# A memory layer's sample keys and values, turned on VectorE and gathered on GpSimd instead of transposed on TensorE

## The chip, the cores and the metric

The kernel runs on one core of one Trainium2 chip. The metric is the device time of one launch in microseconds (us), lower is better; a kernel's time is the median of its runs. The kernel before takes 877.05 us (three runs, 877.02 to 877.51). In what follows PE is TensorE, DVE VectorE, ACT ScalarE, POOL GpSimd and SP SyncE, which here issues loads and stores.

## The reference

One inference step of a two-layer decoder: 256 prompt tokens of one new sequence, and 64 sample tokens (8 sequences of 8 tokens), which carry states along. Layer 0 mixes tokens with a gated MLP, layer 1 with an mLSTM memory of 8 heads (keys of 128, values of 256 numbers); a convolutional FFN follows each. The change lies in layer 1. For each head and chunk the reference computes (cut):

```python
sc  = einsum('bhtd,bhsd->bhts', qc, kc) * w_intra          # scores
num = w_inter[..., None] * einsum('bhtd,bhde->bhte', qc, C) \
    + einsum('bhts,bhse->bhte', sc, vc)
den = w_inter * einsum('bhtd,bhd->bht', qc, n) + sum(sc, -1)
h   = num / maximum(abs(den), exp(-m_t))[..., None]
kg  = kc * g[..., None]
C_new = decay * C + einsum('bhsd,bhse->bhde', kg, vc)      # the state update sums over tokens
```

Then each head's output is normalised, multiplied by `sigmoid(o)` and projected. The state update and `sc @ v` sum over tokens, so that keys and values are needed with tokens on the partitions, while the projections deliver them with features on the partitions.

## The kernel before

All activations lie with features on the 128 partitions and the T = 320 tokens (256 of the prompt, then 64 of the sample) along the row. A weight matrix is worked in output blocks of 128 rows; `block()` multiplies one by up to eight 128-row pieces of the activations in three passes (high part by high part, low by high, high by low), each matmul 128x320 into one PSUM bank. The raw weights come by SP's queue, ACT makes the high part `wh` (line 178), DVE the low part `wl` (line 179). PE runs these passes from the start to the end of the program.

PSUM has eight banks: a ring of three (`psm`, tile `pm`) and one of five (`psa`). A block takes the next bank of `psm`; so does the second matmul of most pairs `pcs` of the state update, and in heads 1 to 6 `pk`. The next owner of a bank waits until the last one's readers are done.

`layer_b` runs over the heads h = 0 to 7. The iteration of head h works on its own projections and finishes head h-1. On PE, for heads 2 to 6: q block, k block, `inter`(h-1) (old state by q), `numer`(h-1) (scores by values), first v block, `state_prompt`(h-1) (`pCp`), a pair `pcs` of the sample's state update, second v block, more `pcs`, `scores`(h) (`psc`), first o block, `pcs`, second o block, `finish`(h-1) (six transposes `phn` of the normalised output, line 1102), `pcs`, then `k_nat`(h) and `v_nat`(h): three transposes of k (`pk`) and six of v (`pv`), two tiles of prompt tokens and one of sample tokens each. Head 1 has its first v block ahead of `inter`, and its first o block ahead of `scores`. Heads 4 to 6 hold eight early blocks of the output projection. Beside it:

- `qk_epi`: scale by the norm (`bpad`), convolution (`bcv`, one step on ACT, three on DVE), Tanh (`bth`), then `qs` (lines 849 and 851, prompt and sample apart), with a second copy of the sample's 64 columns (line 857) for k, and the splits `qh`, `qhl`, `kh`, `khl`.
- `v_epi`: ACT copies a v block from PSUM to `vTb` (line 868), and the sample's columns once more (line 869).
- `scores`: `w`, `Qz`, then `Pf` on DVE, split into `Ph`, `Pl` and, for the sample, `Ps`.
- `v_nat`: `vh` on ACT (line 932), `vl` and the sample's lower half of `vh` on DVE (line 935), `vb` on ACT. `k_nat`: the sample's gated keys `kgs` (961 ACT, 962 DVE), POOL's masked copies `kgz` (985), the prompt's `kgh`, `kgl`.
- `stats`: `dn` on ACT, moments `mv`, then `rd`, `t1` on DVE, `sl` on POOL; `normed`: `nb` on DVE, `hn` on ACT. `state_sample`: DVE adds `pcs` to a state tile `C` (line 1081), SP stores it. `o_epi`: `o_b` on DVE (line 1089), `th_o` on ACT. `finish`: `y_b` on DVE (lines 1105 and 1106, prompt and sample apart), split into `yhb`, `ylb`.

PE's order is the program's, pinned by `mm` and `tr`. On the other engines a scheduler sets it from the dependences, with edges given by hand: `behind(a, b)` puts a after b on their engine without a wait, `issue_after` does so for all that a block of code issues.

Of the kernel before, what the change touches and what calls it, by code (L numbers as in the profile page):

```python
# [11 lines left out]
F32 = mybir.dt.float32  # L12
F32R = mybir.dt.float32r
AF = mybir.ActivationFunctionType
# [17 lines left out]
CW = DV + 2  # L32
HV = 160


# [24 lines left out]
class Net:  # L60
# [627 lines left out]
    def layer_b(self):  # L688
# [5 lines left out]
        with ExitStack() as ctx:  # L694
# [24 lines left out]


            def gates(rp):

# [108 lines left out]
            def qk_epi(h, j, ps):  # L831
# [16 lines left out]
                qs = lp.tile([P, 384], F32, tag="qs", name="qs", bufs=2)  # L848
                q_ = nc.vector.scalar_tensor_tensor(qs[:, :TP], th[:, :TP], 1.0, cv[:, :TP], op0=ADD, op1=MULT)
                tv, c_ = [x[:, 256:].rearrange("p (b e) -> p b e", e=11)[:, :, 3:11] for x in (th, cv)]  # L850
                s["q_"] = q_, nc.vector.scalar_tensor_tensor(seg(qs[:, TP:T]), tv, 1.0, c_, op0=ADD, op1=MULT)
                nm = "kh" if j else "qh"
# [3 lines left out]
                if j:  # L856
                    nc.scalar.copy(qs[:, T:384], qs[:, TP:T])
                if j:
                    self.split(hh, ll, qs[:, :n])
                else:  # L860
                    self.split_y(hh, ll, qs[:, :n])
                s["hi"] = self.parts[0]
                s["qk"[j]] = (qs, hh, ll)
                return self.parts[1]

            def v_epi(h, j, ps):
                vT = lp.tile([P, 384], F32, tag="vT", name="vTb", bufs=2)
                nc.scalar.copy(vT[:, :T], ps[:, :T])
                made = nc.scalar.copy(vT[:, T:384], ps[:, TP:T])
# [9 lines left out]
            def scores(h):  # L879
# [28 lines left out]
                Qd = Qz[:, NS:].rearrange("p (b e) -> p b e", e=32)[:, :, :NS]  # L908
                nc.vector.scalar_tensor_tensor(Qd, seg(q[:, TP:T]), 0.5, seg(pb[:, T:384]), op0=MULT, op1=MULT)
                Pf = hp.tile([P, 448], F32, tag="Pf", name="Pf", bufs=1)  # L910
# [7 lines left out]
                both = Ps.rearrange("p i (j e) -> p i j e", e=32)[:, :, :, :16]  # L918
                nc.scalar.copy(both[64:], both[:64])
                s["P"] = (Ph, Pl, dec)  # L920

            def v_nat(h):
                s = S[h]
                pv = [self.psa.tile([P, 512], F32, tag="pa", name="pv") for _ in range(2)]
                dsts = [pv[t // 2][:, (t % 2) * DV:] for t in range(3)]
                for t in range(3):
                    for e in range(2):
                        self.tr(dsts[t][:, e * P:(e + 1) * P], s["vT"][e][:, t * P:(t + 1) * P], self.ident)
                for t in range(3):
                    dst = dsts[t]  # L930
                    sc = self.rc[:, t:t + 1]
                    nc.scalar.activation(vh[:, t, :, :P], parity(dst[:, :DV]), AF.Copy, scale=sc)

                    r, out = (slice(0, P), vl[:, t, :, :P]) if t < 2 else (slice(64, P), vh[64:, t, :, :P])
                    low = nc.vector.scalar_tensor_tensor(out, parity(dst[r, :DV]), sc[r], vh[r, t, :, :P].bitcast(F32), op0=MULT, op1=SUB)
                    if t == 1:
                        self.v_low = low

                nc.scalar.copy(vb[:, :, :P], vh[:, 2, :, :P])
                self.vb_made = nc.scalar.copy(vb[:32, :, :P], vh[32:64, 2, :, :P])  # L940

            def v_first(h):

                nc.scalar.copy(vh[32:64, 2, :, :P], vh[:32, 2, :, :P])

            def k_nat(h):
# [10 lines left out]
                g = colsT[:, 2, 32 + h:33 + h]  # L957
                src = pk[:, 2 * P:3 * P]

                for i, (r, o) in enumerate(((slice(0, 32), slice(32, 64)), (slice(32, 64), slice(0, 32)))):  # L960
                    nc.scalar.activation(kgs[:, i, :], src, AF.Copy, scale=g)
                    s["ks"] = nc.vector.scalar_tensor_tensor(kgs[o, i, :], src[r], g[r], kgs[r, i, :].bitcast(F32), op0=MULT, op1=SUB)
# [3 lines left out]

                def prompt():
                    for t in range(2):
                        g = colsT[:, t, 32 + h:33 + h]
                        src = pk[:, t * P:(t + 1) * P]  # L970
                        nc.scalar.activation(kgh[:, t, :], src, AF.Copy, scale=g)
                        nc.vector.scalar_tensor_tensor(kgl[:, t, :], src, g, kgh[:, t, :].bitcast(F32), op0=MULT, op1=SUB)

# [4 lines left out]
            def k_mask(h):  # L978
                _, _, kgs, kgz = S[h]["kg"]
                if h == NH - 1:  # L980
                    for b in range(NB):
                        nc.scalar.activation(kgz[:, b, :], kgs[:, b // 4, :].bitcast(F32), AF.Copy, scale=mk[:, b:b + 1])
# [37 lines left out]
            def stats(h, between=None):  # L1020
                s = S[h]
                num, mv, dn = s.pop("num"), mvs[h % 2], dns[h % 2]
                v_first(h)
                for t in range(3):
                    nc.scalar.activation(dn[:, t:t + 1], num[t][:, DV:DV + 1], AF.Abs)
                bst = hp.tile([P, 3, 6], F32, tag="bstat", name="bstat", bufs=1)
                for t in range(3):
                    nc.vector.bn_stats(bst[:, t, :], num[t][:, :DV])
                    nc.vector.bn_aggr(mv[:, t, :], bst[:, t:t + 1, :])
# [6 lines left out]
                sl = hp.tile([P, 3], F32, tag="sl", name="sl", bufs=1)  # L1036
                nc.gpsimd.tensor_tensor(sl, t1, self.mhalf.to_broadcast([P, 3]), op=ALU.pow)
                s["norm"] = num, mv, sl
# [4 lines left out]
            def normed(h):  # L1043
# [5 lines left out]
                for t in range(3):  # L1049
                    if h == NH - 1 and t:  # L1050
                        nc.vector.tensor_scalar(hn[:, t, :], src[t][:, :DV], mv[:, t, 0:1], sl[:, t:t + 1], op0=SUB, op1=MULT)
                    else:
                        nc.scalar.activation(hn[:, t, :], src[t][:, :DV], AF.Identity, scale=sl[:, t:t + 1], bias=nb[:, t:t + 1])
# [41 lines left out]
            def finish(h):  # L1095
# [3 lines left out]
                for e in range(2):  # L1099
                    pt = self.psa.tile([P, 512], F32, tag="pa", name="phn")  # L1100
                    for t in range(3):
                        self.tr(pt[:, t * P:(t + 1) * P], hn[:, t, e * P:(e + 1) * P], self.ident)
                    y = self.tp.tile([P, T], F32, tag="yf", name="y_b", bufs=2)
                    o = s["o"][e]
                    nc.vector.scalar_tensor_tensor(y[:, :TP], o[:, :TP], 1.0, pt[:, :TP], op0=ADD, op1=MULT)
                    nc.vector.scalar_tensor_tensor(pairs(y[:, TP:]), pairs(o[:, TP:]), 1.0, apart(pt[:, TP:384]), op0=ADD, op1=MULT)
                    g = gnh[:, 2 * h + e:2 * h + e + 1]
                    yp, h2, l2 = parity(y), halves(yh[:, e, :]), halves(yl[:, e, :])
                    nc.scalar.activation(h2, yp, AF.Copy, scale=g)
                    s.setdefault("yl", []).append(nc.vector.scalar_tensor_tensor(l2, yp, g, h2.bitcast(F32), op0=MULT, op1=SUB))  # L1110
# [129 lines left out]
            begin(0)  # L1240
            self.prefetch(0, self.used + 2)
            begin(1)
            inter(h)
            numer(h)
            ps = blk()

            def between():
                with tc.issue_after(self.t_made.ins):
                    self.prefetch(0, self.used + 2)
                o_epi(h, 0, ps)  # L1250

# [89 lines left out]
def _lay_out(i):  # L1341
# [28 lines left out]
    w = i["b_w_in"][0]  # L1370
    a["b_win"] = _blocks(w[:, :48 * P], order)
    g = np.zeros((P, 2 * P), w.dtype)
# [64 lines left out]
```

## Time and profile before

| | |
|---|---|
| median of three runs | 877.05 us |
| the profiled execution | 876.92 us, its span 875.2 us |
| memory layer, head 1's q block to head 7's | 412.0 to 587.9 us |
| busy: PE, DVE, ACT, POOL | 869.1, 671.8, 506.0, 143.0 us |
| PE's clock granted | full in all slices |
| one wl split (DVE), one wh split (ACT) | 1.18 and 1.01 us, 254 of each |
| a weight matmul 128x320 | 0.30 us each, one every 0.136 us |

Matmuls overlap in the array: a row of the timeline shows each with its whole duration, and what a matmul costs is the distance to the next one's start. In the timeline a row is: start, duration, engine, line, operation, output <- inputs, shape, count; in brackets stands the idle time before it and what ended it. A busy engine that is never the last to be waited for costs nothing.

### The profile page before, as it was taken

To read this page: it belongs to the slowest core of one execution; us is meant where nothing else is said; L and a number is where in the kernel's file an instruction comes from. 1 tells how busy PE (TensorE), PEld (TensorE's weight loads), DVE (VectorE), ACT (ScalarE), POOL (GpSimd) and SP (SyncE) were. 2 spreads that over 40 slices of the span, in tenths; PEclk is the share of its full clock that TensorE was granted. 3 is DMA by queue.
4 is the path that set the end of the run, shared out by engine and by line. 5 is a ranking of instruction groups with operands and counts; after the bars stand their busy time and mean duration, and the time that the engine had idled before them with its cause. 6 is when DMAs were issued, how large, how long until landed. Compare 5 with 4: busy or idle time off the path is not lost.

```text
span 875.2 us, 16934 instructions
## 1 busy us (share of the span) xinstructions
PE 869.1 (99%) x6388; PEld 852.2 (97%) x6388; DVE 671.8 (77%) x1302; ACT 506.0 (58%) x917; POOL 143.0 (16%) x297
## 2 busy tenths in 40 slices
PE   9999999999999999999999999999999999999997
PEld 7899999999999999999999999999999999999997
DVE  7766986588878865559999997878998888786443
ACT  7557554455555543447877776656766555554442
POOL 3530000031000000005433232313003000000000
PEclk9999999999999999999999999999999999999999
DMA  8855645545445555555746777565664554455551
GB/s 264 259 170 167 183 145 180 170 155 171 156 158 169 162 167 157 158 185 150 241 152 225 242 232 219 184 215 170 197 219 145 170 169 149 165 163 166 156 153 60
DMA packets 54949, 155.74 MB, mean 178 GB/s; under 512 B 7460, under 2 KB 12716, under 8 KB 54868
## 3 DMA queue, kind: packets, MB, share of 16 engines
q1 hardware_dynamic: 54868, 154.67, 55.7%
q8 instruction: 50, 0.82, 0.4%
q14 instruction: 31, 0.25, 0.1%
HBM read 142.66 MB, written 11.99 MB: 177 GB/s over the span
## 4 chain that ended last, share of the span: by engine, by line
PE 99%; DMA 0%; DVE 0%; ACT 0%; POOL 0%; issue 0%
PE pm L81 85%; PE pv_a L81 6%; PE num L81 2%; PE pmix L81 1%; PE pcs L81 1%; PE psc L81 1%; PE pCp L81 1%; PE phn L84 1%; PE pv L84 1%; DMA xT<-in_xv 0%; PE pk L84 0%; DVE y_p L677 0%; PE pg L81 0%; PE pc L81 0%; DVE y_s L684 0%; PE pt L84 0%
## 5 line engine op out<-in xcount | busy, mean ns | idle before, releaser
L179 DVE TENSOR_TENSOR wl<-raw,wh 128x1024 fp32r<-128x1024 f32 (+4 forms) x254 | 299.2, 1179 | 112.4 <-ACT wh L178 111.9
L178 ACT CAST wh<-raw 128x1024 fp32r<-128x1024 f32 (+4 forms) x254 | 255.5, 1006 | 217.9 <-PE pm L81 148.9
L81 PE MATMUL pm<-xh,wh 128*128 128x320 f32 x1216 | 356.1, 300 | 0.0
L81 PE MATMUL pm<-xl,wh 128*128 128x320 f32 x1216 | 354.5, 299 | 0.0
L81 PE MATMUL pm<-xh,wl 128*128 128x320 f32 x1216 | 308.8, 299 | 0.0
L81 PEld LDWEIGHTS pm<-xh,wh 128*128 128x128 f32 x1216 | 229.9, 189 | 0.6 <-issue 0.5
L81 PEld LDWEIGHTS pm<-xl,wh 128*128 128x128 f32 x1216 | 229.9, 189 | 0.0
L81 PEld LDWEIGHTS pm<-xh,wl 128*128 128x128 f32 x1216 | 212.0, 189 | 0.0
L81 PE MATMUL pm<-yh_f,wh 128*128 128x320 f32 x352 | 105.2, 299 | 0.0
L81 PE MATMUL pm<-yl_f,wh 128*128 128x320 f32 x352 | 105.2, 299 | 0.0
L81 PE MATMUL pm<-yh_f,wl 128*128 128x320 f32 x352 | 105.2, 299 | 0.0
L81 PEld LDWEIGHTS pm<-yh_f,wh 128*128 128x128 f32 x352 | 66.5, 189 | 0.0
L81 PEld LDWEIGHTS pm<-yl_f,wh 128*128 128x128 f32 x352 | 66.5, 189 | 0.0
L81 PEld LDWEIGHTS pm<-yh_f,wl 128*128 128x128 f32 x352 | 66.5, 189 | 0.0
L581 DVE SCALAR_TENSOR_TENSOR fcv<-fpad,vecs,fcv 128x336 f32<-128x336 f32 x88 | 49.2, 565 | 1.4
L583 ACT ACTIVATE fgl<-fcv 128x256 f32<-128x256 f32 x44 | 18.2, 415 | 37.2 <-DVE fcv L581 37.2
L81 PE MATMUL pm<-yh_a,wh 128*128 128x320 f32 x128 | 38.4, 300 | 0.0
L81 PE MATMUL pm<-yl_a,wh 128*128 128x320 f32 x128 | 38.3, 299 | 0.0
L81 PE MATMUL pm<-yh_a,wl 128*128 128x320 f32 x128 | 38.3, 299 | 0.0
L323 DVE TENSOR_TENSOR xT<-pm,xT 128x320 f32<-128x320 f32 x39 | 19.1, 489 | 24.2 <-PE pm L81 24.2
L81 PE MATMUL pm<-yhb,wh 128*128 128x320 f32 x128 | 35.9, 304 | 0.0
L81 PE MATMUL pm<-ylb,wh 128*128 128x320 f32 x128 | 35.5, 300 | 0.0
(268 smaller groups left out, 1269.2 us busy)
## 6 DMA issues: line engine op xcount, KB each, us to landing
raw<-in_f_up SPq DMA_DIRECT2D x88, 512.0 KB, 3.5
raw<-in_b_win SPq DMA_DIRECT2D x48, 512.0 KB, 3.9
raw<-in_f_dn SPq DMA_DIRECT2D x32, 448.0 KB, 3.4
C<-in_C SPq DMA_DIRECT2D x32, 258.0 KB, 5.4
out_Cs<-C SPq DMA_DIRECT2D x32, 258.0 KB, 4.3
raw<-in_a_win SPq DMA_DIRECT2D x16, 512.0 KB, 3.7
raw<-in_a_wo SPq DMA_DIRECT2D x16, 512.0 KB, 4.2
raw<-in_f_dn SPq DMA_DIRECT2D x16, 512.0 KB, 3.6
```

Of the source, the lines that this page charges most:

```text
L81: self.pin(self.nc.tensor.matmul(out, lhsT, rhs, start=start, stop=stop, skip_group_check=skip))
L84: self.pin(self.nc.tensor.transpose(out, in_, ident))
L178: self.last_split = self.hold(nc.scalar.copy(wh[:, :kn, :], raw[:, :kn, :]))
L179: self.last_low = nc.vector.tensor_tensor(wl[:, :kn, :], raw[:, :kn, :], wh[:, :kn, :].bitcast(F32), op=SUB)
L323: self.nc.vector.tensor_tensor(x, ps[:, :T], x, op=ADD)
L581: nc.vector.scalar_tensor_tensor(cv, pd[:, i:i + NC], self.vec(w + i * KF), cv, op0=MULT, op1=ADD)
L583: nc.scalar.activation(gl[:, :TP], cv[:, :TP], AF.Gelu_apprx_tanh)
```

## The change

For heads 1 to 6 (`TURNED`), PE transposes only the prompt's tiles of k and v. `turn` does the sample's 64 tokens: DVE turns them in blocks of 32x32 into `kv` (the k block from `ks2`, a copy of the sample's keys written twice, the two v blocks straight from PSUM), and POOL copies the turned blocks into `nat`, with tokens on the partitions: eight copies of 32x32 and one of 64x128 for k, eight of 32x2x32 for v. `kgs` and the sample's `vh` are then made from `nat` in SBUF. ACT's `vTb` copies of v shrink from 320 and 64 columns to one of 256. The columns of v's weights are put in another order on the host, so that a head's even and odd columns are two halves.

For heads 0 to 6, `qs` is made for the padded row of 344 columns in one DVE instruction instead of 256 and 64, the scores of the sample read `ks2`, and the sample's normalised output is transposed by an identity with its columns in another order (`pick`), so that `y_b` is one instruction of 320 columns instead of 256 and 64. Further edges `behind` order the moved work; for the last head they keep an order.

The diff, cut to its core:

```diff
+TURNED = range(1, NH - 1)
...
             def qk_epi(h, j, ps):
...
-                q_ = nc.vector.scalar_tensor_tensor(qs[:, :TP], th[:, :TP], 1.0, cv[:, :TP], op0=ADD, op1=MULT)
-                tv, c_ = [x[:, 256:].rearrange("p (b e) -> p b e", e=11)[:, :, 3:11] for x in (th, cv)]
-                s["q_"] = q_, nc.vector.scalar_tensor_tensor(seg(qs[:, TP:T]), tv, 1.0, c_, op0=ADD, op1=MULT)
+                n = TP if h == NH - 1 else NC
+                s["q_"] = nc.vector.scalar_tensor_tensor(qs[:, :n], th[:, :n], 1.0, cv[:, :n], op0=ADD, op1=MULT),
...
-                if j:
-                    nc.scalar.copy(qs[:, T:384], qs[:, TP:T])
...
+                if j and h < NH - 1:
+                    s["ks2"] = lp.tile([P, P], F32, tag="ks2", name="ks2", bufs=2)
+                    nc.scalar.copy(s["ks2"].rearrange("p (i b e) -> p i b e", i=2, e=NS), twice(qs))
+                    if h in TURNED:
+                        turn(h, 0, s["ks2"][:, :64])
...
             def v_epi(h, j, ps):
                 vT = lp.tile([P, 384], F32, tag="vT", name="vTb", bufs=2)
-                nc.scalar.copy(vT[:, :T], ps[:, :T])
-                made = nc.scalar.copy(vT[:, T:384], ps[:, TP:T])
+                n = TP if h in TURNED else T
+                made = nc.scalar.copy(vT[:, :n], ps[:, :n])
+                if n == T:
+                    made = nc.scalar.copy(vT[:, T:384], ps[:, TP:T])
...
+                if n < T:
+                    turn(h, 1 + j, ps[:, TP:T])
...
+            def turn(h, i, x):
+
+                s = S[h]
+                if not i:
+                    s["kv"] = lp.tile([P, 2, 3, 32], F32, tag="kv", name="kv", bufs=2)
+                    s["nat"] = lp.tile([P, 3, P], F32, tag="nat", name="nat", bufs=2)
+                s.setdefault("turns", []).append(nc.vector.transpose(s["kv"][:, :, i, :], x))
+                a, z = ((0, 1), None, (1, 3))[i] or (0, 0)
+                for c in range(2) if z else ():
+                    for q in range(0, P, 32):
+                        s.setdefault("gathers", []).append(
+                            nc.gpsimd.tensor_copy(s["nat"][32 * c:32 * c + 32, a:z, q:q + 32], s["kv"][q:q + 32, c, a:z, :]))
+                if not i:
+                    nc.gpsimd.tensor_copy(s["nat"][64:, 0, :], s["nat"][:64, 0, :])
...
             def scores(h):
-                mm(sc[:, 384:448], k[:, TP:384], q[:, TP:T], True, True)
+                mm(sc[:, 384:448], s["ks2"], sample_q(h), True, True)
...
             def v_nat(h):
-                for t in range(3):
+                n = 2 if h in TURNED else 3
+                pv = [self.psa.tile([P, 512], F32, tag="pa", name="pv") for _ in range(n - 1)]
+                dsts = [halves(pv[t // 2][:, (t % 2) * DV:(t % 2 + 1) * DV]) for t in range(n)]
+                if n < 3:
+                    dsts.append(s["nat"][:, 1:])
+                for t in range(n):
...
+                    if t == n:
+                        self.behind(made, s["Ps"][0])
...
+                if h == 1:
+                    for first in S[0]["yh"]:
+                        self.behind(first, made)
...
             def k_nat(h):
-                for t in range(3):
-                    self.tr(pk[:, t * P:(t + 1) * P], ks[:, t * P:(t + 1) * P], self.ident)
+                for t in range(2 if h in TURNED else 3):
+                    self.tr(pk[:, t * P:(t + 1) * P], ks[:, t * P:(t + 1) * P] if t < 2 else s["ks2"], self.ident)
...
-                src = pk[:, 2 * P:3 * P]
+                src = s["nat"][:, 0] if h in TURNED else pk[:, 2 * P:3 * P]
...
-                    nc.scalar.activation(kgs[:, i, :], src, AF.Copy, scale=g)
+                    made = nc.scalar.activation(kgs[:, i, :], src, AF.Copy, scale=g)
+                    if h in TURNED:
+                        self.behind(made, s["Ps"][0])
...
             def stats(h, between=None):
...
-                nc.gpsimd.tensor_tensor(sl, t1, self.mhalf.to_broadcast([P, 3]), op=ALU.pow)
+                raised = nc.gpsimd.tensor_tensor(sl, t1, self.mhalf.to_broadcast([P, 3]), op=ALU.pow)
+                if h + 1 in TURNED:
+                    self.behind(S[h + 1]["turns"][0], self.t_made)
+                    self.behind(S[h + 1]["gathers"][0], raised)
...
             def finish(h):
...
-                        self.tr(pt[:, t * P:(t + 1) * P], hn[:, t, e * P:(e + 1) * P], self.ident)
+                        pick = self.ident if t < 2 or h == NH - 1 else self.ident.rearrange("p (j i e) -> p i j e", i=2, e=16)
+                        self.tr(pt[:, t * P:(t + 1) * P], hn[:, t, e * P:(e + 1) * P], pick)
...
```

How it stands in the engines' order. On PE, at the end of head 1 (`phn` are the transposes of head 0's output, `pk` and `pv` those of head 1's k and v), before:

```order
L81 MATMUL pcs<-vh,kgz 128x258 x2
L84 MATMUL phn<-ident,hn 128x128 x6
L81 MATMUL pcs<-vb,kgz 128x258 x2
L84 MATMUL pk<-ident,qs 128x128 x3
L84 MATMUL pv<-ident,vTb 128x128 x6
L81 MATMUL pm<-xh,wh 128x320
```

And now:

```order
L82 MATMUL pcs<-vh,kgz 128x258 x2
L85 MATMUL phn<-ident,hn 128x128 x6
L82 MATMUL pcs<-vb,kgz 128x258 x2
L85 MATMUL pk<-ident,qs 128x128 x2
L85 MATMUL pv<-ident,vTb 128x128 x4
L82 MATMUL pm<-xh,wh 128x320
```

One transpose of k and two of v are gone, in each of heads 1 to 6; nothing else on PE changes its place.

On DVE, in head 1, from the moments of head 0 (`mv`, `rd`, `t`) to head 1's first `o_b`, before:

```order
L849 SCALAR_TENSOR_TENSOR qs<-bth,bcv 128x256
L851 SCALAR_TENSOR_TENSOR qs<-bth,bcv 128x64
L1029 BN_AGGR mv_4933<-bstat 128x2 x2
L1032 TENSOR_TENSOR rd<-dn_4932,cols 128x3
L1081 SCALAR_TENSOR_TENSOR C_4769<-C_4769,dec,pcs 128x258
L334 TENSOR_TENSOR khl<-qs,kh 128x128
L1034 SCALAR_TENSOR_TENSOR t_5137<-rd 128x3
L1081 SCALAR_TENSOR_TENSOR C_4769<-C_4769,dec,pcs 128x258
L1035 SCALAR_TENSOR_TENSOR t_5137<-t_5137,mv_4933 128x3
L909 SCALAR_TENSOR_TENSOR Qz<-qs,Mb 128x8x8
L179 TENSOR_TENSOR wl<-raw,wh 128x1024
L1089 TENSOR_TENSOR o_b<-pm,rb 128x320
```

And now, up to the transpose of the second v block:

```order
L864 SCALAR_TENSOR_TENSOR qs<-bth,bcv 128x344
L1089 BN_AGGR mv_4932<-bstat 128x2 x2
L1092 TENSOR_TENSOR rd<-dn_4931,cols 128x3
L905 STREAM_TRANSPOSE kv<-pm 128x2x32
L1094 SCALAR_TENSOR_TENSOR t_5147<-rd 128x3
L335 TENSOR_TENSOR khl<-qs,kh 128x128
L1095 SCALAR_TENSOR_TENSOR t_5147<-t_5147,mv_4932 128x3
L905 STREAM_TRANSPOSE kv<-ks_5067 128x2x32
L1146 SCALAR_TENSOR_TENSOR C_4768<-C_4768,dec,pcs 128x258 x2
L949 SCALAR_TENSOR_TENSOR Qz<-qs,Mb 128x8x8
L180 TENSOR_TENSOR wl<-raw,wh 128x1024
L905 STREAM_TRANSPOSE kv<-pm 128x2x32
```

The first transpose from `pm` reads the first v block; it stands right behind `rd`. The one from `ks` (the tile `ks2`) stands behind the second step of `t`, the second v block's behind `wl`.

On DVE, the end of head 2 (its two `o_b`, and the state tiles `C` of head 1), before:

```order
L1089 TENSOR_TENSOR o_b<-pm,rb 128x320
L1081 SCALAR_TENSOR_TENSOR C_5272<-C_5272,Mb,pcs 128x258 x2
L179 TENSOR_TENSOR wl<-raw,wh 128x1024
L1089 TENSOR_TENSOR o_b<-pm,rb 128x320
L1105 SCALAR_TENSOR_TENSOR y_b<-th_o,phn 128x256
L1106 SCALAR_TENSOR_TENSOR y_b<-th_o,phn 128x64
```

And now:

```order
L1154 TENSOR_TENSOR o_b<-pm,rb 128x320
L1146 SCALAR_TENSOR_TENSOR C_5290<-C_5290,Mb,pcs 128x258 x2
L1015 SCALAR_TENSOR_TENSOR kgs<-nat,cols,kgs 32x128 x2
L981 SCALAR_TENSOR_TENSOR vh<-nat,rc,vh 64x2x128
L180 TENSOR_TENSOR wl<-raw,wh 128x1024
L1154 TENSOR_TENSOR o_b<-pm,rb 128x320
L1172 SCALAR_TENSOR_TENSOR y_b<-th_o,phn 128x320 x2
```

`kgs` and the sample's `vh`, which followed `pk` and `pv` behind the second `o_b`, now stand ahead of it; in head 1 one `kgs` does, right behind `Ps`.

More of the change, by code (lines that the diff above doesn't have):

```diff
@@ L718, in apart, with sample, sample_q, twice @@
                 return x.rearrange("p (j e) -> p j e", e=32)[:, :, :16]
+            def sample(x):
+                return x[:, TP:NC].rearrange("p (b e) -> p b e", e=11)[:, :, 3:]
+            def sample_q(h):
+                q = S[h]["q"][0]
+                return sample(q) if h < NH - 1 else seg(q[:, TP:T])
+            def twice(x):
+                return sample(x).unsqueeze(1).to_broadcast([P, 2, NB, NS])
             def gates(rp):
@@ L942, in v_first @@
             def v_first(h):
-                nc.scalar.copy(vh[32:64, 2, :, :P], vh[:32, 2, :, :P])
+                return nc.scalar.copy(vh[32:64, 2, :, :P], vh[:32, 2, :, :P])
             def k_nat(h):
@@ L981, in k_mask @@
                     for b in range(NB):
-                        nc.scalar.activation(kgz[:, b, :], kgs[:, b // 4, :].bitcast(F32), AF.Copy, scale=mk[:, b:b + 1])
+                        self.behind(nc.scalar.activation(kgz[:, b, :], kgs[:, b // 4, :].bitcast(F32), AF.Copy, scale=mk[:, b:b + 1]), self.dn_made)
                     return
@@ L1022, in stats @@
                 num, mv, dn = s.pop("num"), mvs[h % 2], dns[h % 2]
-                v_first(h)
+                first = v_first(h)
+                if h == NH - 1:
+                    self.behind(first, self.kg_parts[2])
                 for t in range(3):
-                    nc.scalar.activation(dn[:, t:t + 1], num[t][:, DV:DV + 1], AF.Abs)
+                    self.dn_made = nc.scalar.activation(dn[:, t:t + 1], num[t][:, DV:DV + 1], AF.Abs)
+                    if h == NH - 1:
+                        self.behind(self.dn_made, first)
                 bst = hp.tile([P, 3, 6], F32, tag="bstat", name="bstat", bufs=1)
                 for t in range(3):
-                    nc.vector.bn_stats(bst[:, t, :], num[t][:, :DV])
+                    made = nc.vector.bn_stats(bst[:, t, :], num[t][:, :DV])
+                    if h == NH - 1:
+                        self.behind(made, self.kg_parts[3])
                     nc.vector.bn_aggr(mv[:, t, :], bst[:, t:t + 1, :])
@@ L1245, in layer_b @@
             ps = blk()
+            self.behind(self.last_low, self.kg_parts[1])
             def between():
```

44 lines of the change are left out of this document (29 added, 15 removed).

## The prediction

> **What bounds the kernel now.** I read the page's busy table and its chain of waits first, then the memory layer head by head as busy time in windows (heads are called by their index h; the turned ones, "two to seven", are h = 1 to 6).
>
> ```profile
> PE 869.1 (99%) x6388; PEld 852.2 (97%) x6388; DVE 671.8 (77%) x1302; ACT 506.0 (58%) x917; POOL 143.0 (16%) x297
> PE 99%; DMA 0%; DVE 0%; ACT 0%; POOL 0%; issue 0%
> 412.00:438.40 26.40, 26.40 (x216) 25.54 (x214) 24.75 (x61) 22.15 (x57) 10.99 (x25) 1.00 0.72 229
> 438.40:464.40 26.00, 26.00 (x211) 25.24 (x209) 25.73 (x66) 19.62 (x47) 8.62 (x13) 1.00 0.58 194
> 464.40:490.40 26.00, 26.00 (x211) 25.24 (x208) 23.94 (x61) 19.36 (x46) 7.43 (x13) 1.00 0.68 230
> 490.40:516.40 26.00, 26.00 (x210) 25.24 (x208) 23.94 (x61) 19.37 (x46) 7.37 (x13) 1.00 0.71 222
> 516.40:552.10 35.70, 35.70 (x281) 34.94 (x280) 28.98 (x67) 22.60 (x49) 9.40 (x13) 1.00 0.68 217
> 552.10:587.90 35.80, 35.80 (x283) 35.04 (x281) 29.09 (x67) 22.67 (x49) 9.20 (x12) 1.00 0.63 201
> ```
>
> The columns after the window and its length are PE, PEld, DVE, ACT and POOL busy, the granted clock, DMA share and GB/s. The six windows run from the first matmul of one head's q block to the next head's, h = 1 to 6. TensorE (PE) is never idle in them, at clock 1.00, and the chain of waits is PE to 99%: whatever PE no longer does is time saved, and whatever PE is made to wait for is time lost. But the average hides a second limit: VectorE (DVE), 77% over the span, is 24.75 of 26.40 us busy in head 1, 25.73 of 26.00 in head 2, 23.94 in heads 3 and 4, and has over 6 us to spare only in heads 5 and 6, which carry extra output-projection blocks.
>
> **What the change removes.** Each turned head loses one transpose of k and two of v on PE.
>
> ```profile
> 586.96 0.49 PE L84 MATMUL pk<-ident,qs 128*128 128x128 f32 x3
> 587.29 0.82 PE L84 MATMUL pv<-ident,vTb 128*128 128x128 f32 x6
> 587.86 0.38 PE L81 MATMUL pm<-yhb,wh 128*128 128x320 f32 x1
> ```
>
> Matmuls overlap, so the price is the pitch, not the duration: three transposes lead from 586.96 to 587.29, 0.33 us, 0.109 each. Eighteen are **-1.96 us**, 0.33 per head. The scores matmul that now reads ks2 keeps its width, and the head's output transposes only read the identity in another order: nothing on PE.
>
> [...]
>
> **What it puts on VectorE.** Three 64-column stream transposes per head (v0, ks2, v1). Rows of that operation exist only at 320 columns (0.51 us); the 64-column operations below take 0.21, and follow each other by 0.13 to 0.14.
>
> ```profile
> L315 DVE STREAM_TRANSPOSE rb<-nr 128x320 f32<-128x320 f32 x4 | 2.0, 512 | 0.1
> 430.26 0.40 DVE L849 SCALAR_TENSOR_TENSOR qs<-bth,bcv 128x256 f32<-128x256 f32 x1
> 430.58 0.21 DVE L851 SCALAR_TENSOR_TENSOR qs<-bth,bcv 128x64 f32<-128x64 f32 x1
> 430.72 0.24 DVE L1029 BATCH_NORM_AGGREGATE mv<-bstat 128x2 f32<-128x6 f32 x2
> 430.88 0.13 DVE L1032 TENSOR_TENSOR rd<-dn,cols 128x3 f32<-128x3 f32 x1
> ```
>
> I take 0.21 (bounds 0.13 and 0.51): 0.4 to 0.6 us per head. The joined qs (two per head) and y_b (two) give back four 64-column operations at about 0.13, 0.5 us. VectorE's work is thus about level, and ScalarE's two copies of v fewer are no term, as it has 4 us or more to spare in each window. What counts is the **order**.
>
> **Term 1, a wait in head 1.** A block's PSUM bank comes from a ring of three, which the second matmul of most pcs pairs uses too; head 1's o0 block gets v0's bank. Before, ScalarE alone emptied it:
>
> ```profile
> 426.72 0.43 ACT L868 COPY vTb<-pm 128x320 f32<-128x320 f32 x1
> 427.03 0.22 ACT L869 COPY vTb<-pm 128x64 f32<-128x64 f32 x1
> 428.81 0.30 PE L81 MATMUL pm<-xh,wh 128*128 128x320 f32 x1
> ```
>
> It was free at 427.25, 1.56 us before o0's first matmul at 428.81. Now VectorE's transpose of v0 must read it too, and in the new order that stands behind rd. In head 1 VectorE runs without a gap, and the rows above put it at rd at 430.88. That gives rd's start + 0.13 + 0.13 to 0.21, about 431.15, and o0 at 431.2: PE stands **2.4 us**, after a block that nothing delayed. The joined qs may bring it forward by 0.1 or 0.2. This wait alone is more than the 1.96.
>
> **Term 2, the end of head 1.** VectorE's second wait-chain then runs late:
>
> ```profile
> 432.77 0.47 PE L81 MATMUL pcs<-vh,kgz 128*128 128x258 f32 x2
> 436.33 0.39 PE L81 MATMUL pcs<-vh,kgz 128*128 128x258 f32 x2
> 433.33 0.47 DVE L1089 TENSOR_TENSOR o_b<-pm,rb 128x320 f32<-128x320 f32 x1
> 433.73 0.86 DVE L1081 SCALAR_TENSOR_TENSOR C<-C,dec,pcs 128x258 f32<-128x258 f32 x2
> 434.52 0.15 DVE L1046 SCALAR_TENSOR_TENSOR nb<-mv,sl 128x3 f32<-128x3 f32 x1
> 434.70 1.02 ACT L1053 ACTIVATE hn<-num,nb,sl 128x256 f32<-128x256 f32 x2 [0.39 <-DVE nb L1046]
> 436.75 0.30 ACT L919 CAST Ps<-Ps 64x128 fp32r<-64x128 f32 x1
> 436.53 0.49 DVE L1089 TENSOR_TENSOR o_b<-pm,rb 128x320 f32<-128x320 f32 x1
> 437.41 0.87 DVE L1081 SCALAR_TENSOR_TENSOR C<-C,dec,pcs 128x258 f32<-128x258 f32 x2
> 438.40 0.38 PE L81 MATMUL pm<-xh,wh 128*128 128x320 f32 x1
> ```
>
> The last matmul is head 2's q block. Its bank is freed by the C pair at 437.41, done at 438.28: even before, only 0.12 us of slack, so that head 1 could not have kept its 0.33 in any case. In the new order kgs<-nat (0.34 by its group below) stands ahead of the second o_b, and ScalarE's kgs ahead of that, behind the copy of Ps. With o0 2.4 later, PE does the next pcs pair at 435.16 instead of 432.77. Its C pair starts about 435.5, nb comes near 436.3 (+1.8), so the copy of Ps at 436.75 + 1.8 = 438.55, ScalarE's kgs to 438.95 or 439.1, VectorE's to 439.4; o_b starts at about 439.5, where 438.9 would be possible by the matmuls (o1's end, 436.33, 2.4 later, and a handover). From o_b to the q block were 438.40 - 436.53 = 1.87 us, 1.75 to the end of the C pair: the q block starts at about 441.3, **+2.9** on 438.40 with head 1's saving already in it. Bounds: +2.35 (o_b at 438.9 and the short distance, 440.75) and +3.2 (later handovers).
>
> **Term 3, head 2.** Here kgs twice and the sample's vh move ahead of the second o_b:
>
> ```profile
> L962 DVE SCALAR_TENSOR_TENSOR kgs<-pk,cols,kgs 32x128 fp32r<-32x128 f32 x16 | 5.5, 341 | 0.5
> L935 DVE SCALAR_TENSOR_TENSOR vh<-pv,rc,vh 64x256 fp32r<-64x256 f32 x8 | 3.9, 491 | 0.3
> 462.87 0.49 DVE L1089 TENSOR_TENSOR o_b<-pm,rb 128x320 f32<-128x320 f32 x1
> ```
>
> They are 2 x 0.34 + 0.49 = 1.17 us. The next q block waits for that o_b's read, done at 463.36, and starts at 464.40: 1.04 us of slack, 0.71 when PE has three transposes less. A VectorE that works 25.73 of 26.00 us cannot catch up elsewhere, so 1.17 - 0.71 = 0.46 waits, with a handover 0.5: net **+0.2** after the saving. Bounds -0.33 (it fits) and +0.8 (nothing of the slack is left).
>
> **Term 4, heads 3 to 6.** In 3 and 4 VectorE has 2.06 us to spare, in the same order of work; I let waits eat half to two thirds of their 0.66, net **-0.2** (bounds -0.66 and 0). In 5 and 6 it has 6.7, and they keep all: **-0.66**. The v and k turns of heads 2 to 6 themselves cost no wait by my walk: their banks are wanted after two blocks or more.
>
> **Sum** at the end of head 6: 2.9 + 0.2 - 0.2 - 0.66 = **+2.25**. Everything behind shifts with it. The profiled execution took 876.92 us (span 875.2 and 1.7 around it), 0.13 under the median of 877.05, so 877.05 + 2.25 = **879.3**.
>
> **GpSimd and the ports.** Seventeen copies per head have no row; the nearest:
>
> ```profile
> 425.18 1.26 POOL L900 TENSOR_SCALAR_AFFINE_SELECT w<-w 64x64 f32<-64x64 f32 x1
> 432.22 1.91 POOL L1037 TENSOR_TENSOR sl<-t,mhalf 128x3 f32<-128x3 f32 x1 [2.29 <-DVE t L1035]
> 499.81 0.20 POOL L836 COPY bpad<-bst 128x24 f32<-128x24 f32 x1
> 499.95 0.20 POOL L839 COPY bns<-bpad 128x24 f32<-128x24 f32 x1
> 424.98 1.31 DVE L179 TENSOR_TENSOR wl<-raw,wh 128x1024 fp32r<-128x1024 f32 x1
> 432.19 1.21 DVE L179 TENSOR_TENSOR wl<-raw,wh 128x1024 fp32r<-128x1024 f32 x1
> ```
>
> Undisturbed they follow by 0.14; one that meets VectorE's wl (424.98 to 426.29) lasts until wl ends, and that wl took 0.10 more than the next. So nine k gathers cost 1.3 us if free, some 4 with three wl met. In head 1 they start when sl is raised (434.13 before), and kgs wants them near 438.7: just in time, no term; 1.5 us later if each met something. What VectorE loses in return, 0.1 at a time, is 0.2 or 0.3 per head, inside the bounds.
>
> [...]
>
> **Rivals.**
> - **Late gathers** (slower): each of the first nine copies meets a wl or another two-input operation, 0.6 us apiece, nine done at 439.4 to 440 instead of 438.7; o_b in heads 1 and 2 is 0.8 later each: 2.25 + 1.6 = +3.9, 880.9. For: the 1.26. Against: most copies beside VectorE work took 0.2 to 0.4. It decides from 0.5 us per copy. Chance 0.15.
> - **Only the first wait counts**: o0's 2.4 stays, but the ends of heads 1 to 4 fit, since later starts leave VectorE its slack: 2.4 - 1.96 = +0.4, 877.5. For: o_b possible at 438.9. Against: the 0.12 us of slack. Chance 0.25.
> - **The turn comes in time** (faster): VectorE takes v0's bank before o0 wants it; then -1.96 if no end is late, 875.1. For it VectorE would have to be at rd 2.4 us sooner, and its rows leave no gap. Chance 0.07.
>
> **How the numbers follow.** My forecast, 879.3, has 0.53, and its own range by the terms' bounds is 877.8 to 880.4. Low, 876.9, is just under the second case; high, 881.2, just over late gathers. A measurement here tells 0.2%, 1.75 us, from no change: faster is under 875.3, slower over 878.8. Slower takes the late gathers and most of the forecast, 0.61; same takes the second case and the forecast's lower end, 0.31; faster 0.08.
>
> **What would show it.** PE idle before o0 of head 1, near 428.8, for 2 to 2.5 us, ended by VectorE's stream transpose; idle again before head 2's q block, ended by a C update; under 0.6 in head 2; none in heads 5 and 6, which should each be 0.33 shorter than 35.7 and 35.8. GpSimd's k gathers done before VectorE's kgs in head 1. Wrong would make it: the transpose of v0 ahead of rd in time, PE idle in heads 5 and 6, or a transpose from PSUM far over 0.5 us.

## The result, and the profile after

The changed kernel takes **882.5 us** (median of 6 runs, 881.99 to 883.27), the kernel before 877.04 in the same sitting: 5.5 us slower, ratio 1.0062 (95% interval 1.0051 to 1.0073). The forecast was 879.3, at most 881.2: the direction was right, the size too small by more than half.

The page of the changed kernel, busy times and the chain that ended last, and then its waits on TensorE (PE): engine and line that waited, what released it, us in total, times, the longest.

```profile
PE 870.6 (99%) x6370; PEld 852.4 (97%) x6370; DVE 674.5 (77%) x1292; ACT 503.8 (57%) x905; POOL 174.8 (20%) x399
PE 91%; DVE 5%; ACT 1%; DMA 1%; issue 1%; POOL 1%; DVEq 0%
```

```profile
PE pm L82 <- DVE t L1094: 2.2, 1, 2.2
PE pm L82 <- DVE o_b L1154: 1.7, 3, 1.1
...
PE pm L82 <- DVE C L1146: 0.4, 1, 0.4
PE pk L85 <- DVE o_b L1154: 0.3, 1, 0.3
```

Eighteen matmuls are gone and the chain, PE to 99% before, now runs through VectorE (DVE) for 5%. But these waits are 4.6 us; less the 1.96 saved, they explain 2.6 of 5.5. Much of the rest shows where the clock is read. Windows of the changed kernel (window, length, then PE, PEld, DVE, ACT, POOL busy, granted clock, DMA share, GB/s):

```profile
428.29:431.70 3.41, 1.26 (x10) 1.05 (x9) 3.41 (x17) 1.64 (x4) 0.58 (x2) 1.00 0.97 370
431.70:435.11 3.41, 3.41 (x15) 3.41 (x14) 1.90 (x5) 0.64 (x3) 3.06 (x10) 0.50 0.86 313
435.11:438.52 3.41, 3.41 (x28) 3.41 (x28) 1.88 (x6) 1.84 (x3) 2.02 (x9) 1.00 0.38 135
```

After the window in which PE stood idle for most of the time, the clock was granted at half for 3.41 us. PE is 100% busy there, and 15 matmuls fall in it, where 28 fall in the window behind. The timeline shows the same: a pitch of 0.27 us in place of 0.136.

```profile
431.03 0.37 PE L82 MATMUL pm<-xh,wh 128*128 128x320 f32 x1 [2.15 <-DVE t L1094]
431.24 0.30 PE L82 MATMUL pm<-xl,wh 128*128 128x320 f32 x1
...
432.12 0.47 PE L82 MATMUL pm<-xh,wh 128*128 128x320 f32 x1
432.38 0.47 PE L82 MATMUL pm<-xl,wh 128*128 128x320 f32 x1
...
436.04 0.27 PE L82 MATMUL psc<-qh,kh 128*128 128x256 f32 x1
```

Setting PE's instructions of both profiled executions side by side by start gives where the time went; the changed one is 0.09 us ahead when it comes to head 1 and 5.94 behind after head 6:

| place | forecast | measured |
|---|---|---|
| PE idle before o0 of head 1 | +2.4 | +2.31 |
| half clock behind it | none | +1.75 |
| end of head 1, its saving included | +0.5 | +0.72 |
| head 2, net | +0.2 | +1.00 |
| heads 3 and 4, net | -0.2 | +0.56 |
| heads 5 and 6, net | -0.66 | -0.31 |
| sum | +2.25 | +6.03 |

Heads are cut here at the first matmul behind a head's transposes of v. For heads 5 and 6 that is the first of two early blocks, not the q block, which starts 6.6 us later (522.95 for head 5 in the kernel before). The windows ahead of the forecast, said to run from q block to q block, have the same edge, and the first of them begins within a block (head 1's q block starts at 410.16, not 412.0). Each still holds the moved transposes of one head, so the saving is read rightly.

### The profile page after: what moved, and what is told of

Same layout as the page of the kernel before. It is cut to its first block, busy times and chain, and to the rows that moved or that the text cites. A ratio compares the mean times of both kernels' runs of the same rounds, so it can differ in the third digit from the quotient of the medians.

```text
span 881.1 us, 16970 instructions
## 1 busy us (share of the span) xinstructions
PE 870.6 (99%) x6370; PEld 852.4 (97%) x6370; DVE 674.5 (77%) x1292; ACT 503.8 (57%) x905; POOL 174.8 (20%) x399
## 4 chain that ended last, share of the span: by engine, by line
PE 91%; DVE 5%; ACT 1%; DMA 1%; issue 1%; POOL 1%; DVEq 0%
PE pm L82 79%; PE pv_a L82 6%; PE num L82 2%; DVE wl L180 2%; PE pmix L82 1%; DMA raw<-in_b_win 1%; DVE bcv L859 1%; PE pcs L82 1%; PE pCp L82 1%; PE psc L82 0%; PE pw L82 0%; PE phn L85 0%; DVE C L1146 0%; DVE o_b L1154 0%; ACT wh L179 0%
## 5 line engine op out<-in xcount | busy, mean ns | idle before, releaser
L577 POOL COPY fns<-fpad 128x2 f32<-128x2 f32 x44 | 12.4, 281 | 138.1 <-DVE fpad L573 137.7
```

The costliest lines, as they stand in the source:

```text
L577: nc.gpsimd.tensor_copy(nst[:, b, 16:18], pd[:, 256:258])
```

## The experiments

All start from the changed kernel. "Before" ran beside each of them: 876.92 to 877.11.

**x1: the v blocks of head 1 turned from a copy.** The bank of v0 then waits for ScalarE (ACT) alone, as before the change; VectorE's transposes keep their place.

```diff
             def v_epi(h, j, ps):
-                n = TP if h in TURNED else T
+                n = TP if h in TURNED and not (h == 1) else T
...
-                    turn(h, 1 + j, ps[:, TP:T])
+                    turn(h, 1 + j, (ps if n < T else vT)[:, TP:T])
```

> Head 1 alone: ScalarE copies all 320 columns of both v blocks, and VectorE turns them from that copy in SBUF; its place in VectorE's order stays, only the PSUM bank no longer waits for it. Theory (the bank of v0 is held by VectorE's place in line, and the half clock of 3.4 us follows from PE's 2.3 us of idle): o0 starts at 428.7 again, no clock below 1.00 between 430 and 436, and the 2.31 and 1.75 us go, with most of the 0.8 at the end of head 1: 878.0 (877.5 to 878.5). Rival (PE waits there for something else of the change, such as GpSimd's copies slowing VectorE): the idle time stays, 882 to 882.5. Second rival (the slow matmuls are not due to the idle time): the 2.31 goes, the 0.267 us pitch stays, 880.

Measured: 880.32 (880.21 to 881.92); 878 was expected. The idle time before o0 is gone, so the bank was what PE waited for. The second rival had named 880 too, but its slow matmuls are not there: in the profiled execution o0 runs at a pitch of 0.136 us and a clock of 1.00. But half of the gain came back at the end of head 1. The timeline of x1 there, VectorE first, then GpSimd (POOL):

```profile
437.89 0.34 DVE L1015 SCALAR_TENSOR_TENSOR kgs<-nat,cols,kgs 32x128 fp32r<-32x128 f32 x1 [0.93 <-ACT kgs L1012]
438.26 0.49 DVE L1154 TENSOR_TENSOR o_b<-pm,rb 128x320 f32<-128x320 f32 x1
438.67 1.19 DVE L335 TENSOR_TENSOR Pl<-Pf,Ph 128x384 fp32r<-128x384 f32 x1
439.78 0.86 DVE L1146 SCALAR_TENSOR_TENSOR C<-C,dec,pcs 128x258 f32<-128x258 f32 x2
```

```profile
438.40 1.04 POOL L1039 TENSOR_TENSOR kgz<-kgs,mk 128x512 fp32r<-128x512 f32 x1 [0.44 <-DVE kgs L1015]
```

Two things hold PE. kgs stands ahead of o_b and waits 0.93 us for ACT, so o_b comes at 438.26 instead of 436.53. And Pl takes 1.19 us instead of 0.55: kgz, which needs kgs and so comes earlier than before the change, has just begun on GpSimd, and Pl ends 0.4 after it. The C pair, on which head 2's q block waits, is late by both: PE waits 0.8 us (`pk`, for o_b) and 1.0 us (the q block, for the C pair). Before the change Pl stood there too, with kgz far behind it:

```profile
436.94 0.55 DVE L334 TENSOR_TENSOR Pl<-Pf,Ph 128x384 fp32r<-128x384 f32 x1
440.44 1.04 POOL L985 TENSOR_TENSOR kgz<-kgs,mk 128x512 fp32r<-128x512 f32 x1
```

The profiled execution of x1 is the longest of its six (881.92; four took 880.21 to 880.33). These two waits fall in one window there, and the clock is halved in the next, in head 2's q block:

```profile
438.08:441.49 3.41, 1.67 (x12) 1.44 (x13) 3.38 (x8) 3.20 (x8) 1.33 (x2) 1.00 0.05 19
441.49:444.90 3.41, 3.41 (x15) 3.41 (x14) 3.35 (x8) 1.71 (x6) 0.95 (x3) 0.50 0.43 157
```

**x2: vh behind o_b in heads 2 to 4.** In `v_nat`, for these heads:

```diff
+                        if h in (2, 3, 4):
+                            self.behind(made, s["o_th"])
...
+                    if t == n and h in (2, 3, 4):
+                        self.behind(low, s["o_ob"])
```

> In heads 2, 3 and 4 the sample's part of vh, made from nat, is put behind the second th_o on ScalarE and behind the second o_b on VectorE; all else as changed. Theory (PE's waits of 1.09, 0.25 and 0.49 us before the q blocks of heads 3, 4 and 5 come from o_b standing behind a vh that waits for GpSimd's last gathers): they go, 1.5 to 1.8 us, 880.8. Rival (VectorE has too much work in these heads, wherever vh stands): the waits stay, 882.0 to 882.5. The wait before o0 of head 1 stays in both.

Measured: 880.82 (880.39 to 881.17), as expected. The three waits are gone from PE. The changed kernel's head 2 shows why they were there; POOL, ACT and DVE:

```profile
459.61 3.72 POOL L910 COPY nat<-kv 32x32 f32<-32x32 f32 x8
463.39 0.64 POOL L912 COPY nat<-nat 64x128 f32<-64x128 f32 x1
464.09 3.21 POOL L910 COPY nat<-kv 32x64 f32<-32x64 f32 x8
```

```profile
467.33 0.51 ACT L976 ACTIVATE vh<-nat,rc 64x256 fp32r<-64x256 f32 x1 [1.92 <-POOL nat L910]
```

```profile
467.88 0.48 DVE L981 SCALAR_TENSOR_TENSOR vh<-nat,rc,vh 64x256 fp32r<-64x256 f32 x1 [0.68 <-ACT vh L976]
468.39 1.23 DVE L180 TENSOR_TENSOR wl<-raw,wh 128x1024 fp32r<-128x1024 f32 x1
469.53 0.48 DVE L1154 TENSOR_TENSOR o_b<-pm,rb 128x320 f32<-128x320 f32 x1
```

The seventeen copies take 7.7 us and end at 467.30. Taken one by one, most last 0.20 or 0.23 us and follow each other by 0.24 or 0.27, which would make 4.4 us. But three of them met a wl on VectorE and lasted until it ended (0.83, 1.36 and 1.25 us), and the 64x128 copy, beside Pl, took 0.64 instead of 0.29. One of the three, and its wl:

```profile
461.97 1.36 POOL L910 COPY nat<-kv 32x32 f32<-32x32 f32 x1
462.05 1.20 DVE L180 TENSOR_TENSOR wl<-raw,wh 128x1024 fp32r<-128x1024 f32 x1
```

ACT's vh waits for the copies, VectorE's vh for ACT's, wl and o_b stand behind, and PE's q block behind o_b.

That the measured time agrees with the expected 880.8 to 0.02 is partly luck: the four times lie in two pairs, about 880.5 and 881.1, and the profiled execution (880.52) had no half clock, while its wait for the C pair before head 2's q block grew from 0.4 to 1.3 us. By the starts on PE, the layer takes 1.8 us less than in the changed kernel from that q block on; that is what this edit gives.

**x3: both edits.**

> Both edits together. If the two theories are right and independent, 882.5 - 4.4 - 1.7 = 876.4, and no lower than the sum without any wait, 877.05 - 1.96 = 875.1. If one repaired wait only uncovers the next: 877 to 879.

Measured: 878.69 (878.37 to 880.14), not 876.4: the wait at the end of head 1 is uncovered, as in x1. Its ten times fall into two groups, six from 878.37 to 878.88 and four from 879.99 to 880.14; the profiled execution is of the upper one, at a mean clock of 0.998, and has a half clock in head 2's q block.

**x4: the idle time filled.** Eighteen matmuls nobody reads, ahead of o0 of head 1:

```diff
             def state_prompt(h):
...
+                self.spare = pc[:, CW:512], kgh[:, 0, :], self.xh[:, 0, :512 - CW]
...
                 if h == 1:
+                    for _ in range(18):
+                        mm(*self.spare, True, True)
                     o_epi(h, 0, blk())
```

> The changed kernel with 18 further matmuls (128x254, results into unused columns of a bank, read by nobody) ahead of o0 of head 1, about 2.0 of the 2.3 us that PE stands idle there. Theory (the clock is halved for a window because PE stood idle): o0 starts when it did, the clock stays 1.00, and the 1.75 us go: 880.8. Rival (the matmuls are slow because of what runs beside them, or because o0's operands come late): the pitch of 0.267 us stays, 882.5 or a little more.

Measured: 882.19 (882.11 to 882.48). The half clock is gone (the first o_b, behind o0, starts at 434.66 us instead of 436.24), so the idle time had caused it; but only 0.3 us of 1.75 went with it by the medians, and 0.7 between the two profiled executions. In x4's timeline Pl meets kgz as in x1; VectorE, then GpSimd:

```profile
440.15 1.43 DVE L335 TENSOR_TENSOR Pl<-Pf,Ph 128x384 fp32r<-128x384 f32 x1
440.13 1.04 POOL L1039 TENSOR_TENSOR kgz<-kgs,mk 128x512 fp32r<-128x512 f32 x1 [2.54 <-PE pcs L82]
```

In the changed kernel Pl began first, by 0.01 us; it took 0.55, and kgz was the one that lasted longer:

```profile
441.70 0.55 DVE L335 TENSOR_TENSOR Pl<-Pf,Ph 128x384 fp32r<-128x384 f32 x1
441.71 1.44 POOL L1039 TENSOR_TENSOR kgz<-kgs,mk 128x512 fp32r<-128x512 f32 x1 [4.22 <-PE pcs L82]
```

What PE won by its clock, VectorE lost again before the C pair. Hence the next three.

**x5: kgs later in head 1.** x3, and in `k_nat` of head 1 (`late` is the C pair behind the second o_b):

```diff
+                        if h == 1:
+                            self.behind(made, s["o_th"])
...
+                    if h == 1:
+                        self.behind(s["ks"], s["late"])
```

> x3_both, and head 1's kgs behind the second th_o on ScalarE and behind the C pair that follows the second o_b on VectorE. Theory (with the first wait gone, what is left in head 1 is o_b and Pl standing behind kgs, 0.93 + 1.07 us of waits, and a window of half clock, 1.57, that these two waits bring about): all three go, 878.69 - 3.57 = 875.1, 0.2% under the kernel before. Rival (VectorE is too full in heads 1 and 2 to let PE be 0.33 us faster per head): PE waits again at the next o_b or C pair, 876.5 to 877.5.

Measured: 878.06 (877.82 to 878.36), above the theory's 875.1 and the rival's range: PE is on time to the end of head 1, then waits 1.0 us before head 3's q block (o_b, behind two kgs), 0.3 for a wl and 0.5 in the first early block behind head 4's transposes. Moving kgs takes both its own wait and kgz out of Pl's way; which of the two was worth how much is read from the rows above, not shown by a run.

**x6 and x7: the price of the first wait.** x6 is x5 without x1's edit, x7 the same with x4's matmuls.

> The changed kernel with vh later (heads 2 to 4) and kgs later (head 1), but VectorE's turn of v0 from PSUM where the change puts it: of all waits only the one before o0 of head 1 is left. It prices that wait in the open: 875.1 + 2.3 = 877.4 in an execution without a half clock behind it, 879.0 with one (1.57 to 1.75 more). If the end of head 1 is late whatever comes before it, 878.5 to 880 also without a half clock.

> x6_first_wait_only with the 18 idle-time matmuls of x4_fill ahead of o0. Theory (x4_fill came out only 0.3 under the changed kernel because the time it saved was lost again to kgs and Pl at the end of head 1, not because the half clock costs nothing): no half clock, 877.4 to 877.6, and up to 1.6 under x6_first_wait_only. Rival: no difference between the two.

Measured: x6 881.28 (880.16 to 881.88), x7 879.71 (879.61 to 880.16). Both are 2 us above what was expected, for what x5 showed of the heads behind. The differences stand: the idle time itself costs 879.71 - 878.06 = 1.7 us, the half clock **1.57** more once the end of head 1 is no longer late by itself. Windows of x6, then of x7:

```profile
429.68:433.09 3.41, 1.40 (x10) 1.43 (x11) 3.41 (x17) 2.20 (x5) 1.26 (x4) 1.00 0.95 313
433.09:436.50 3.41, 3.41 (x15) 3.41 (x14) 1.17 (x2) 1.04 (x1) 2.98 (x10) 0.50 0.95 308
```

```profile
427.90:431.30 3.40, 3.40 (x28) 3.23 (x27) 3.40 (x16) 1.23 (x5) 0.21 (x1) 1.00 0.92 293
431.30:434.70 3.40, 3.40 (x27) 3.40 (x27) 2.44 (x7) 2.05 (x3) 3.07 (x8) 1.00 0.99 379
```

**x8: the packing alone.** `TURNED = ()`: no head is turned.

> No head is turned: the joined qs and y_b, ks2, the padded queries and the other order of v's columns stay; PE has all its transposes again. Theory (the packing alone changes nothing on PE, and VectorE's 0.5 us per head is not waited for): 877.0, within 0.3 of the kernel before. Rival (part of the loss sits in the packing, through ScalarE's copy into ks2 or the longer qs): 878 to 880.

Measured: 877.20 (877.02 to 878.99) against 876.97, ratio 1.0004 (0.9995 to 1.0014). The joined rows, the padded queries and the other order of the columns cost and bring nothing that can be told from no change; the loss is in the turning.

**x10, x11: kgs and kgl later too.** x5, with kgs of heads 2 to 4 behind y_b; x11 also with head 1's second kgl behind the wl that PE waited for.

```diff
+                    if h in (2, 3, 4):
+                        self.behind(made, s["o_th"])
+                        self.behind(s["ks"], s["y_b"])
...
-                        for low in (*S[0]["yl"], S[1]["ks"]):
+                        for low in (*S[0]["yl"], S[1]["ks"], self.kg_parts[3]):
```

> x5_kgs_later, and in heads 2 to 4 kgs too goes behind the second th_o (ScalarE) and behind y_b (VectorE). Theory (the 1.05 us before head 3's q block and the slow start of head 4's early block, 0.47, are o_b and ylb standing behind two kgs): both go, 878.06 - 1.5 = 876.5. Rival (VectorE simply has 1 us too much to do in heads 2 to 4): PE waits the same at the next piece, 877.7 to 878.1.

> x10_kgs_later_all, and in head 2's q block the weights' low part wl ahead of the second kgl, which waits for ScalarE. Theory: the wait of 0.28 us at 444.3 goes as well, 876.2 (bounds 875.1, the sum without any wait, and 876.6): all of the change's transposes at most 0.2% under the kernel before. Rival: no difference to x10_kgs_later_all.

Measured: 878.03 and 878.07 (for x11 ratio 1.0011, 1.0002 to 1.0020): no gain over x5, the rival's result. The large waits are gone, and PE is late by the same amount in pieces of 0.1 to 0.25 us at scores, o_b and early blocks. x11's windows by head (the stretch of the q blocks of heads 2 to 5):

```profile
438.60:464.80 26.20, 26.05 (x204) 24.89 (x204) 25.97 (x61) 18.37 (x43) 16.93 (x30) 1.00 0.53 165
464.80:491.10 26.30, 26.09 (x205) 25.00 (x205) 24.66 (x60) 18.52 (x43) 14.22 (x31) 1.00 0.80 265
491.10:517.40 26.30, 26.09 (x205) 25.02 (x205) 24.66 (x60) 18.64 (x43) 14.18 (x30) 1.00 0.70 215
```

PE had 26.00 us a head before and, with three transposes less, would need 25.67; it takes 26.2 to 26.3. VectorE's busy time in heads 3 and 4 is 24.66 instead of 23.94, beside a GpSimd that is busy for 14.2 us instead of 7.4.

**x12: from head 2 on.** `TURNED = range(2, NH - 1)`, with vh and kgs later in heads 2 to 4.

> Only heads 2 to 6 are turned (fifteen transposes, 1.64 us), with kgs and vh later in heads 2 to 4; head 1 keeps PE's transposes and no turn. If head 1 was the place of most of the loss and the later order repairs heads 2 to 4: 877.0 - 1.6 = 875.4 (to 876.2). If VectorE's and GpSimd's load in heads 2 to 4 is too much in any order: 877.

Measured: 876.68 (876.51 to 877.29), ratio 0.9998 (0.9989 to 1.0007): no difference from before, near the rival. By the starts on PE, head 2 keeps its 0.33 and head 3 only 0.06, as the q block behind it comes late; from there to the early blocks behind head 4's transposes PE falls behind by 0.86, more than all that was saved; heads 5 and 6 keep theirs.

**x13: heads 5 and 6 only.** `TURNED = (5, 6)`, in the change's own order.

> Only heads 5 and 6 are turned, in the change's own order: six transposes, 0.66 us, in the two heads where VectorE has over 6 us to spare and where the changed kernel's trace shows no wait. Theory (the turn pays where VectorE keeps pace): 876.9 - 0.66 = 876.3, two heads 0.33 shorter each and no new wait. Rival (the gathers or the turn cost PE something there too): 876.9 or more.

Measured: 876.22 against 876.96, 0.7 less, as expected; by the interval, 0.9983 to 1.0001, not told from no change. But each of its eleven times (876.70 at most) lies under each of the fourteen beside it (876.87 at least), and the profile shows the place: the two heads take 35.35 and 35.43 us, 35.70 and 35.80 before, and PE waits nowhere in them.

```profile
516.40:551.75 35.35, 35.35 (x279) 34.59 (x277) 29.97 (x68) 23.04 (x48) 14.29 (x31) 1.00 0.65 201
551.75:587.18 35.43, 35.43 (x279) 34.67 (x278) 29.89 (x66) 22.45 (x46) 12.19 (x30) 1.00 0.67 203
```

## Why the prediction was right or wrong

- **The saving** was as forecast: 0.33 us per head where nothing waits (x13, and heads 5 and 6 of x12).
- **Term 1** was right in place, cause and length: 2.31 us for 2.4 forecast. VectorE's rows in the changed kernel, which the forecast put at 430.88 and 431.0:

```profile
430.59 0.13 DVE L1092 TENSOR_TENSOR rd<-dn,cols 128x3 f32<-128x3 f32 x1
430.64 0.24 DVE L905 STREAM_TRANSPOSE kv<-pm 128x64 f32<-128x64 f32 x1
```

  The transpose took 0.24 us and the next instruction followed by 0.16, near the 0.21 taken. (The waits name `t`, the instruction behind it.) x1 shows that it was the bank.
- **The first step that failed** is what terms 1 and 2 put behind PE's wait. Head 2's q block was to come 2.9 us late, 3.2 at most, and came 4.8 late. PE's idle time was priced at its own length, but in the profiled execution it also halved the clock for 3.41 us, 1.75 by the ledger: "clock 1.00" was read from a kernel that never stops, and taken for a constant. That alone does not explain the miss: where the clock stayed full, the q block still came 4.0 (x4) and 4.2 us late (x2): in x4 Pl then met kgz (1.43 us instead of 0.55), in x2 PE's wait for the C pair grew to 1.3. How much of the half clock stays thus depends on what comes behind: 1.57 in x6 and x7, 0.7 in the changed kernel's profiled execution against x4's, 0.3 in the medians. Without it the kernel still takes 882.2 (x4), more than the 881.2 of the forecast's upper end.
- **Term 2** had the right chain (kgs ahead of o_b, then the C pair); its part of the end of head 1 was +0.5 by the forecast and +0.72 in this execution. With the half clock away it was +1.64, since Pl then met kgz (x4: 1.43 instead of 0.55). The forecast's rows leave Pl out, which stands between o_b and the C pair, and it asked what a GpSimd instruction meets on VectorE only for the copies, not for kgz, which the change moves ahead.
- **Term 3, the second step that failed**, was mis-sized: +0.2 forecast, +1.00 measured. It counted the work of kgs and vh, 1.17 us, but not that vh waits 0.68 us more for the last gathers. The rival of late gathers had the cause, copies that last until the wl they meet has ended (0.83, 1.36 and 1.25 us in head 2), but the wrong place: it watched the nine copies for k in head 1, of which one met a wl (1.11 us) and which were done at 435.31, well before kgs; in head 2 the eight for v came last. The forecast also had undisturbed copies follow each other by 0.14; here it was 0.24 to 0.27. x2 puts the term, with heads 3 and 4, at 1.7 to 1.8, about as much as the first step.
- **Term 4** failed too for heads 3 and 4: +0.56 instead of -0.2. A gap of 2 us per head on VectorE isn't room for PE to run ahead: x11 and x12, with the order mended, still lose those heads' saving. That VectorE's chain through mv, nb, hn, Ph, Pl and o_b sets the pace there is read from the traces (Pl waits 1.35 us for ACT's Ph in head 4 of x12), not shown by a run that shortens it. In heads 5 and 6 it was right but for the 0.35 lost in the first early block behind head 4's transposes.
- **The other rivals**: the ends of heads 1 to 4 didn't fit, so "only the first wait counts" was wrong; "the turn comes in time" was wrong as argued.

The 882.5 is thus the first wait, the half clock behind it, kgs and Pl in head 1, and vh behind the gathers in heads 2 to 4. They aren't a sum: a later wait takes back what an earlier one gives (by the medians x1 gave 2.2 of 4.06, x4 0.3 of 1.75).

## What to carry to other kernels

Work taken off the busiest engine pays only where the engines that take it over keep pace: look at each stage's own slack, and at which waits end with 0.1 us to spare, before counting the saving. A buffer given one more reader is released at that reader's place in line, so ask first where that is. And an idle time on TensorE can cost more than its length, here 1.57 us more (x6 against x7): add up the idle time near it, and look at the granted clock behind it. Last, an instruction that is moved earlier gets new neighbours: look at what runs beside it there, as kgz beside Pl.

## What the runs showed of the hardware that was not expected

In the changed kernel's trace the granted clock goes to half at 431.70 us and back to full at 435.11. The half clock lasted 3.413 us, the full clock 426.67 us ahead of it and 443.73 behind it, 125 and 130 times as long. The windows here are therefore 3.41 us long; where no change of the clock is near, as in x2 and x4, their edges are an estimate of the author's, whole multiples of 3.413 us from the changes elsewhere in the trace. The window ahead of the half clock in three runs, and two windows of runs in which no half clock followed (in x2 the single gap was even longer, 2.45 us, but by that estimate an edge between windows cut it in two, 1.69 and 0.76):

| kernel | PE idle in the window | clock in the next |
|---|---|---|
| the changed kernel | 2.31 us | 0.50 |
| x6 | 2.01 | 0.50 |
| x1, two shorter waits together | 1.88 | 0.50 |
| x2 | 1.69 | 1.00 |
| x4 | 1.40 | 1.00 |

Idle time is counted here from the pitch's end to the next start. What follows an idle time between 1.69 and 1.88 us no run shows, and that it is the sum within one window that counts is the author's reading of these five. x2's two windows:

```profile
427.10:430.51 3.41, 1.88 (x14) 1.64 (x13) 3.41 (x9) 1.52 (x7) 0.38 (x2) 1.00 0.84 258
430.51:433.92 3.41, 2.65 (x19) 2.68 (x20) 3.33 (x14) 1.91 (x5) 2.26 (x4) 1.00 1.00 361
```

The wait before o0 is thus followed by a half clock in the changed kernel's trace, where an edge lies at 428.29, and by none in x2's, where one lies at 430.51 by the estimate. That the edges fall elsewhere in each execution would fit x3's two groups of times, and each run's mean granted clock goes with it: by its length a half clock alone takes 0.002 off it (half of 3.41 us in 878), and the six short times have 0.999 or 1.000, the four long ones, the profiled one among them, 0.998. The changed kernel's six times show it less sharply: 881.99 to 882.24 at 0.998 or 0.999, 882.77 to 883.27 at 0.997.

GpSimd's copies of 32x32 and 32x64 followed each other by 0.24 and 0.27 us, against 0.14 for the 128x24 copies before, and the three that met a wl in head 2 ended 0.07 to 0.10 us after it. VectorE's Pl, meeting a kgz that had begun 0.3 us earlier, took 1.19 us instead of 0.55 and ended 0.4 after it (x1); behind a kgz ahead by 0.02 it took 1.43 (x4). With Pl ahead by 0.01, Pl took its 0.55 and kgz 1.44 instead of 1.04 (the changed kernel). In these three meetings the one that began later took longer. One row fits less well: the copy at 461.97 began 0.08 us before its wl by the profile, and took 1.36 us all the same.
